# Own tokens' q, g and i as seven block products on two pairs of token blocks, with one written order for five engines

## The chip, the cores and the metric

One Trainium2 chip, one of its cores. The metric is the device time of one launch in microseconds (us); lower is better. TensorE is called PE below, VectorE DVE, ScalarE ACT, GpSimd POOL, and SyncE, whose queue issues most transfers, SP. Matrix work is done in float32 precision by splitting each float32 operand into a high and a low part of a shorter format and adding three products: high times high, high times low, low times high.

## The reference

One layer of a mixed attention and recurrence model on 2048 own tokens and 256 context tokens, width 1024:

```
hx = modulate(rmsnorm(x, g_norm1), mx[0], mx[1])        # (2048, 1024)
hc = modulate(rmsnorm(ctx, g_norm1), mc[0], mc[1])      # (256, 1024)
px = split(hx @ w_in);  pc = split(hc @ w_in)           # w_in: (1024, 3328)
#   columns: q 512, k 128, v 128, hq 512, i 512, ff 512, fb 512, g 512
qx = apply_rope(rmsnorm(heads(px.q), g_q), cos, sin)
kx = apply_rope(rmsnorm(heads(px.k), g_k), cos, sin);  kc = rmsnorm(heads(pc.k), g_k)
att = softmax attention of qx over all keys (context and own)
hg  = bidirectional HGRN2 recurrence of (hq, i, ff, fb), read out with rmsnorm and silu(g)
x = x + mx[2] * (concat(att, hg) @ w_out)
x = x + mx[5] * swiglu(modulate(rmsnorm(x, g_norm2), mx[3], mx[4]), w_gu, w_down)
return rmsnorm(x, g_final)
```

`mx` and `mc` are six vectors each of `silu(c) @ w_mod + b_mod`. The change touches the product with `w_in` and what is done to q and k on the way out of it; the stages behind it stay as they are.

## The kernel before

**Stages.** First comes an opening in which the tokens are loaded, normalised, modulated and transposed into `hT` (features on the partitions, tokens along the row), with high part `hTh` and low part `hTl`. There are five token blocks: block 0 holds the 256 context tokens, blocks 1 to 4 hold 512 own tokens each. Then come the projection steps, one for each group of 256 columns of `w_in`; then attention and recurrence, the output projection, and the feed-forward part (whose first half is already done with seven block products, line 1785).

**A projection step.** `load_raw` (lines 204 to 212) loads 256 columns of all 1024 rows into `ws`. The pool `wst` behind it has one buffer, which the chunks of `w_mod` (`wm`, line 412, 1 MB each) share. `split_w` (lines 214 to 222) makes the high part `wh` on ACT (line 218) and the low part on DVE (line 221) into one of two places that alternate. Then PE runs in one of two forms. `mm_cols` (line 435) holds a 128x128 block of weights and streams tokens: three matmuls of 512 columns for each of the eight row groups (256 columns for the context block). It serves hq and f (the two gate groups ff and fb together). `mm_rows` (lines 438 to 449) holds 128 tokens and streams weights: line 442 sends high and low weights together past `hTh` (512 columns), line 448 the high weights past `hTl` (256 columns). It serves k and v (`kv`), q, g and i. The result is `both` (lines 451 to 454): ACT copies one half out of the accumulator, DVE adds the other.

**Beside the products.** `qk_side` (lines 533 to 605) takes a tile of 128 tokens of q (four heads of one half) or k: it reads the raw product back from DRAM, squares it, sums it (line 553), takes the root on POOL (line 131), multiplies (lines 557 and 558), applies the rotary table (line 567 on DVE four times, line 571 on POOL, line 572), splits high and low (lines 576 and 577), transposes it on PE (line 584) and stores it with two transfers (line 587). `mod_chunk` (lines 409 to 428) makes 256 of the modulation values: a 1 MB load, eight DVE operations `macc` (lines 415 and 417), one matmul, one add, one store. `first_maxima` (lines 607 to 640) finds the first head group's bound for the softmax. A function `pump` moves these along, one step of each at a time, between the product tiles.

**Order.** The opening and block 0 to 4 with kv and hq0 come first. Then the steps are q0, q1, hq1, g0, g1, f0, f1, f2, f3, i0, i1, and in these only PE follows a written order; the others are placed by the scheduler. `first_maxima` runs in i1. Behind i1 the attention stage begins, in which all five engines follow a written order: its first loads are `qa` (line 1144) and `K` (line 1393), its first matmul is `mx` (line 1159).

Of the kernel before, what the change touches and what calls it, by code (L numbers as in the profile page):

```python
# [16 lines left out]
P = 128  # L17
D = 1024
KT = D // P
# [12 lines left out]
NEV = 5  # L32
# [35 lines left out]
def block_kernel(ctx: ExitStack, tc: tile.TileContext, a: dict, out: bass.AP, dbg=None):  # L68
# [24 lines left out]
    s_m0 = dram("s_m0", [4, P])  # L93
    s_att = [dram(f"s_att{j}", [256, T]) for j in range(2)]
# [109 lines left out]
    def load_raw(i, pieces):  # L204

        ws = wst_p.tile([P, KT, 256], F32, tag="wst", name=f"ws{i}")
        o = 0
        for c0, n in pieces:
            nc.sync.dma_start(ws[:, :, o:o + n],
                              a["w_in"][0, :, c0:c0 + n].rearrange("(k p) c -> p k c", p=P))  # L210
            o += n
        return ws

    def split_w(i, ws, wp):

        whl = wp.tile([P, KT, 2, 256], F32R, tag="wh", name=f"wh{i}")
        wh, wl = whl[:, :, 0, :], whl[:, :, 1, :]
        nc.scalar.activation(wh, ws, AF.Copy)
        for q in range(4):
            ks = slice(2 * q, 2 * q + 2)  # L220
            (nc.vector if q % 2 or i > 1 else nc.gpsimd).tensor_tensor(
                wl[:, ks, :], ws[:, ks, :], f32v(wh[:, ks, :]), op=ALU.subtract)
        return wh, wl, whl
# [85 lines left out]
    with proj as st:  # L309
        w_pools = [w_left, w_right]  # L310
        hTp = pool(st, "hT")
        ev = pool(st, "ev", NEV)
        sm = pool(st, "sm", 4)
        sizes = [256, 512, 512, 512, 512]
        hT = [None] * 5
        for b in (4, 3, 1, 2):
            hT[b] = [hTp.tile([P, KT, sizes[b]], F32R, name=f"hT{w}{b}") for w in "hl"]
        ps_mm = pool(st, "ps_mm", 4, PSUM)
        nchunk = [1]
        turned = [None]  # L320

        def load_w(pieces):
# [3 lines left out]
            return split_w(i, load_raw(i, pieces), w_pools[i % 2])  # L326

        first = [early_w]
        with ExitStack() as p1:
            ps_x = pool(p1, "ps_x", 4, PSUM)  # L330
            xh = pool(p1, "xh", 3)
            for gr in list(range(1, NTOK // 256)) + [0]:
                if gr == 0:
                    xp.close()
                    hTc = pool(st, "hTc", side="right")
                    hT[0] = [hTc.tile([P, KT, 256], F32R, name=f"hT{w}0") for w in "hl"]
# [42 lines left out]
                def split_h(kk, hv, eng):  # L379

                    hi = hT[b][0][:, 2 * kk:2 * kk + 2, o:o + 256]
                    hd = nc.scalar.activation(hi, hv, AF.Copy)
                    return hd, eng.tensor_tensor(hT[b][1][:, 2 * kk:2 * kk + 2, o:o + 256], hv, f32v(hi), op=ALU.subtract)
# [14 lines left out]
        ps_t = pool(st, "ps_t", 2, PSUM)  # L398
        ps_q = pool(st, "ps_q", 2, PSUM)
# [3 lines left out]
        gqk = qp.tile([P, 2, 64], F32, name="gqk")  # L403
        nc.sync.dma_start(gqk[:, 0, :], rows_bcast(a["g_q"]))
        nc.sync.dma_start(gqk[:, 1, :], rows_bcast(a["g_k"]))

# [1799 lines left out]
```

## Time and profile before

| what | value |
|---|---|
| median of 3 runs | 3110.42 us (3109.52 to 3111.95) |
| the profiled execution's own time | 3117.9 us |
| its span, first to last instruction | 3116.1 us |
| granted PE clock, mean | 0.996 |
| busy: PE, DVE, ACT, POOL | 99%, 59%, 42%, 51% |
| the 16 DMA engines, mean | 132 GB/s |

PE is busy nearly all the time, so time can be gained by giving it less to do, and is lost wherever something else keeps it waiting. The share of PE at 99% hides that the other engines' load differs from stage to stage. Times in the views are measured from the start of the span. "Idle before" an operation names what ended that idle time.

### The profile page before, as it was taken

The numbers are of one execution on the slowest core, as the hardware profiler recorded it, in microseconds if no ns is written. First come the engines' busy times: TensorE is split into PE (matmuls) and PEld (weight loads), VectorE is DVE, ScalarE is ACT, GpSimd is POOL, SyncE is SP. The second block draws the span as 40 slices with busy tenths as digits, with TensorE's granted clock in tenths as the row PEclk, the third lists the DMA queues.
The fourth block names the chain that finished last, engine by engine and source line by source line (L and its number), as shares of the span: only waits on it lengthen the run. The fifth ranks groups of instructions, "written<-read, shape, count | busy, mean of one in ns | idle before, by whom it ended". The sixth has DMA issues, their size and how long they took to land.

```text
span 3116.1 us, 51235 instructions
## 1 busy us (share of the span) xinstructions
PE 3074.8 (99%) x18844; PEld 2483.8 (80%) x18844; DVE 1845.9 (59%) x3252; ACT 1303.1 (42%) x2656; POOL 1602.7 (51%) x1291
## 2 busy tenths in 40 slices
PE   9999999999999999999999999999999999999999
PEld 7888888886777778777778878788888788888887
DVE  4554655427777787786745574544478743333567
ACT  4422322214545545555553253333345533333454
POOL 3311212106989888898862118676600277776122
PEclk9999999999999999999999999999999999999999
DMA  7544544425111212111124444656596533333765
GB/s 244 159 139 127 155 139 150 141 69 138 42 38 49 67 53 71 39 52 48 42 83 147 129 142 155 213 176 211 171 331 196 182 118 106 102 102 102 254 195 196
DMA packets 372998, 410.77 MB, mean 132 GB/s; under 512 B 34469, under 2 KB 264073, under 8 KB 372234
## 3 DMA queue, kind: packets, MB, share of 16 engines
q1 hardware_dynamic: 369722, 405.06, 41.0%
q8 instruction: 148, 2.42, 0.3%
q10 hardware_dynamic: 3024, 2.43, 0.2%
q14 instruction: 104, 0.85, 0.1%
HBM read 277.54 MB, written 133.97 MB: 132 GB/s over the span
## 4 chain that ended last, share of the span: by engine, by line
PE 70%; DVE 7%; DMA 5%; POOL 3%; issue 2%; ACT 1%; SPq 1%; POOLq 0%; DVEq 0%; ACTq 0%
PE pA L1785 13%; PE av L1215 7%; PE pB L1785 6%; PE y L1355 6%; PE pd0A L2082 4%; PE pd1A L2082 3%; PE s L1190 3%; PE s L1191 3%; PE pC L1785 3%; PE mx L1159 3%; PE i L442 2%; DVE mn L1161 2%; PE pd0B L2082 2%; PE pd1B L2082 2%; PE pa L818 2%
## 5 line engine op out<-in xcount | busy, mean ns | idle before, releaser
L1194 ACT ACTIVATE p<-s 128x512 f32<-128x512 f32 x576 | 338.2, 600 | 372.6 <-PE s L1191 358.1
L1161 DVE TENSOR_REDUCE mn<-mx 128x1 f32<-128x512 f32 x496 | 337.0, 689 | 175.2 <-PE mx L1159 172.3
L1215 PE MATMUL av<-p,VS 128*64 128x256 f32 x2304 | 259.9, 379 | 0.0
L1190 PE MATMUL s<-qa,K 128*128 128x512 f32 x576 | 244.1, 424 | 1.2 <-ACT p L1194 1.0
L1191 PE MATMUL s<-qb,KB 128*128 128x512 f32 x576 | 226.9, 394 | 0.0
L1215 PEld LDWEIGHTS av<-p,VS 128*64 128x64 f32 x2304 | 160.4, 137 | 75.3 <-issue 1.1
L1205 POOL TENSOR_TENSOR ps<-p,p 128x1024 f32<-128x1024 f32 x64 | 153.4, 2396 | 101.8 <-ACT p L1194 101.7
L1159 PE MATMUL mx<-K,qa 128*128 128x512 f32 x496 | 200.1, 404 | 2.4 <-DVE mn L1161 1.2
L435 PE MATMUL f<-hTh,wh 128*128 128x512 f32 (+1 forms) x640 | 188.1, 373 | 0.2 <-ACT ft L475 0.2
L1205 POOL TENSOR_TENSOR ps<-ps,p 128x1024 f32<-128x1024 f32 x64 | 153.1, 2392 | 12.0 <-ACT p L1194 10.6
L2019 DVE TENSOR_TENSOR dl<-dl,x 128x512 fp32r<-128x512 f32 x154 | 113.8, 765 | 66.5 <-ACT x L2012 64.9
L2012 ACT ACTIVATE x<-dl 128x512 fp32r<-128x512 f32 x154 | 95.9, 631 | 95.4 <-DMA dl<-s_hid0S 37.7
L852 POOL TENSOR_TENSOR Q<-Q,T 128x512 f32<-128x512 f32 x96 | 131.3, 1383 | 8.1 <-PE pa L818 7.7
L435 PEld LDWEIGHTS f<-hTh,wh 128*128 128x128 f32 x640 | 116.9, 190 | 20.4 <-ACT ft L475 0.3
L1190 PEld LDWEIGHTS s<-qa,K 128*128 128x128 f32 x576 | 109.0, 189 | 27.0 <-issue 12.3
L2012 ACT ACTIVATE dh<-dl 128x512 fp32r<-128x512 f32 x154 | 88.9, 624 | 98.7 <-PE pd1A L2082 42.2
L2019 DVE TENSOR_TENSOR dl<-dl,dh 128x512 fp32r<-128x512 f32 x154 | 105.5, 697 | 39.9 <-ACT dh L2012 37.7
L1159 PEld LDWEIGHTS mx<-K,qa 128*128 128x128 f32 x496 | 93.6, 189 | 38.0 <-DVE mn L1161 15.3
L131 POOL TENSOR_TENSOR rs_xf<-ms_xf,mhalf 128x1 f32<-128x1 f32 x16 | 9.9, 620 | 221.1 <-DVE ms_xf L129 218.5
L1191 PEld LDWEIGHTS s<-qb,KB 128*128 128x128 f32 x576 | 109.3, 190 | 14.9
L435 PE MATMUL f<-hTl,wh 128*128 128x512 f32 (+1 forms) x320 | 118.7, 371 | 0.0
L131 POOL TENSOR_TENSOR rs_qq<-ms_qq,mhalf 128x4 f32<-128x4 f32 x32 | 34.0, 1061 | 161.0 <-DVE ms_qq L129 160.3
(436 smaller groups left out, 8913.5 us busy)
## 6 DMA issues: line engine op xcount, KB each, us to landing
w<-in_w_gu_dram SPq DMA_DIRECT2D x88, 512.0 KB
wm<-in_w_mod_dram SPq DMA_DIRECT2D x24, 1024.0 KB
dl<-s_wT SPq DMA_DIRECT2D x88, 256.0 KB
dl<-s_wB SPq DMA_DIRECT2D x66, 256.0 KB
wq<-in_w_down_dram SPq DMA_DIRECT2D x44, 256.0 KB
s_wT<-wq SPq DMA_DIRECT2D x44, 256.0 KB
dl<-s_hid1S SPq DMA_DIRECT2D x44, 256.0 KB
dl<-s_hid0S SPq DMA_DIRECT2D x44, 256.0 KB
```

Source lines behind the costliest of these rows:

```text
L435: nc.tensor.matmul(pm[:, :n], w[wi][:, k, c0:c0 + P], hT[b][hi][:, k, :], start=(k == 0 and i == 0), stop=(k == KT - 1 and i == 2))
L1159: nc.tensor.matmul(s, self.qa[:, h * P:(h + 1) * P], K[:, k * 512:(k + 1) * 512], start=True, stop=True)
L1161: nc.vector.tensor_reduce(self.mn[:, h, k:k + 1], s, axis=AX.X, op=ALU.min)
L1190: nc.tensor.matmul(s, KS[self.g][:, ks], self.qa, start=True, stop=False)
L1191: nc.tensor.matmul(s, KB[k // 6][:, k % 6 * P:(k % 6 + 1) * P], self.qb, start=False, stop=True)
L1194: nc.scalar.activation(self.pairs[p][:, o:o + 512], s, AF.Exp, scale=-1.0)
L1205: (nc.gpsimd if SUMS[p] in "PQ" else nc.vector).tensor_tensor(t, a, self.pairs[p], op=ALU.add)
L1215: nc.tensor.matmul(self.av[i * 64:(i + 1) * 64, :256], VS[k // 6][:, k % 6, :], self.pairs[k // 2][:, o:o + 256], start=(k == 0), stop=(k ...
L1355: nc.tensor.matmul(py, m[:, k, :], wo[k][w][hf], start=(k == 0 and i == 0), stop=(k == KT - 1 and i == 2), skip_group_check=True)
L1785: nc.tensor.matmul(acc, w[wi][:, k, :], x[xi][k], start=(start and k == 0 and i == 0), stop=(stop and k == KH - 1 and i == 2), skip_group_ ...
L2019: nc.vector.tensor_tensor(lo, f32v(lo), f32v(hi), op=ALU.subtract)
L2082: nc.tensor.matmul(cur[t], l[:, t * P:(t + 1) * P], r, start=(start and j == 0 and f == 0), stop=(stop and j == NHF - 1 and f == 2), skip_ ...
```

## The change

Own tokens' q, g and i (six groups of 256 columns) are no longer made by `mm_rows` one group at a time. Two groups of 256 columns, the two halves of the 1024 rows and two blocks of 512 tokens form a 2 by 2 by 2 block product, which is done with seven products instead of eight (the scheme that the feed-forward part uses). The weight blocks are A, their sums S1 to S4; the token blocks are B, their sums T1 to T4. Each product has 512 rows of weights, 512 tokens, 256 columns, again in three high and low parts.

- `hT` is now kept as places of half a block (four row groups, 512 tokens, high and low). T1 to T4 take over places of the blocks they are made from, so the raw blocks 1 and 2 are first stored to DRAM (`s_tok`, eight transfers of 1 MB during kv and hq0) and are loaded back when the first pair is done.
- Order of the steps: hq1, f0, f1, f2, then the context's i (two steps of two tiles), then f3, then the first pair (blocks 3 and 4) with q, g, i, then the second (blocks 1 and 2) with q, i, g. Each of these six chunks has seven phases of two slots: 84 slots. A slot is two token tiles of four row groups of three matmuls with 256 columns (line 880).
- From f3 on, PE, DVE, ACT, POOL and SP all follow one written order, built from a table of slots. Weight sums run on POOL (line 838), highs on ACT (line 845), lows on DVE (line 851). Token sums run half on DVE and half on POOL (line 731), with highs on ACT (line 737) and lows on DVE (line 740). They are written for slots -4 to 6 and 38 to 52.
- Results are gathered by an ACT copy (line 967) and DVE adds (line 972). g is finished by Silu on ACT (line 860) and the multiplication by `g_hg` on POOL (line 862). Results are stored from ACT's queue (line 701).
- `g_q`, `g_k` and the constants are multiplied into the rotary table (`gtab`, line 563) once for each tile of 128 tokens, the separate multiplication by `gqk` goes, the four rotary operations on DVE become two (line 580), and the small operation ahead of the root moves to POOL (line 568).
- `first_maxima` runs in the last chunk. The number of evacuation buffers goes from 5 to 4.

Core of the diff:

```diff
-        steps = [None, None,
-                 (jobs_q, 0, ones_of(C_Q)), (jobs_q, 1, ones_of(C_Q + 256)),
-                 (jobs_hq, 1, ones_of(C_HQ + 256)),
-                 (jobs_g, 0, ones_of(C_G)), (jobs_g, 1, ones_of(C_G + 256))]
-        steps += [(jobs_f, h, [(C_FF + h * P, P), (C_FB + h * P, P)]) for h in range(NH)]
-        steps += [(jobs_i, c, ones_of(C_I + c * 256)) for c in range(2)]
+        steps = [(jobs_hq, 1, ones_of(C_HQ + 256))] + [(jobs_f, h, pieces_f(h)) for h in range(NH - 1)]
+        steps += [(context_i, c, ones_of(C_I + c * 256)) for c in range(2)] + [(jobs_f, NH - 1, pieces_f(NH - 1))]
...
+        for i, (f, c, _) in enumerate(steps[:-1]):
+            allowed[0] = 10 + 2 * i
             for n, _ in enumerate(f(c, w)):
...
+                if n == 1:
+                    settle()
                     wn = load_w(steps[i + 1][2])
+                if n >= 1:
+                    pump()
+                    if f is not context_i:
+                        pump()
...
+        chunks = [(pair, ch) for pair, chs in ((1, [chunk_q, chunk_g, chunk_i]), (0, [chunk_q, chunk_i, chunk_g]))
+                  for ch in chs]
+        phases = [("A11", "B11", "A", True, False), ("A12", "B21", "C", True, True), ("S1", "T1", "B", True, False),
+                  ("S2", "T2", "A", False, False), ("S4", "B22", "B", False, True), ("S3", "T3", "A", False, False),
+                  ("A22", "T4", "A", False, True)]
...
+            for t in (2 * u, 2 * u + 1):
+                dst, ts = acc[:, t % 2 * 256:(t % 2 + 1) * 256], slice(t * P, (t + 1) * P)
+                for k in range(H):
+                    for i, (v, f) in enumerate(((vh, 0), (vh, 1), (vl, 0))):
+                        nc.tensor.matmul(dst, v[:, k, ts], w[:, k, f, :],
...
+            summed_at, high_at = (tail_(j - 3), head(j - 2)) if j > 2 else (-4, (-4, 0, 0)[j])
+            if phases[m][0] in SUMS_W:
+                at(summed_at, SUM, weight_sum, c, phases[m][0])
+            at(high_at, HIGH, weight_high, j)
+            at(high_at + 1, LOW, weight_low, j)
...
+        for k in (-4, -4, -3, -3, -2, -2, -1, -1, 0, 1, 2, 3, 4, 5, 6):
+            at(k, TURN, turn)
+        for k, v in ((1, ("B11",)), (3, ("B21",)), (5, ("B12", "T1")), (9, ("B22",))):
+            at(SWITCH + k, LOAD, fetch_tokens, *v)
+        for k in range(10, 25):
+            at(SWITCH + k, TURN, turn)
```

The written order moves instructions at three places that the prediction speaks of.

First, DVE between the context's i and f3. `wh7` and `wh8` are the split weights of two steps that follow each other (`_0` and `_1` are halves), `ws7` and `ws8` the raw ones, `macc16` the modulation chunk that is made from the load `wm16`. Before, at the beginning of f0, where `wh8` serves the next step, f1:

```order
L454 TENSOR_TENSOR ge1_17_4193<-ge1_17_4193,g1_17_4176 128x256
L129 TENSOR_SCALAR ms_qq0_12_4438<-ssq0_12_4436 128x4
L557 TENSOR_TENSOR eq0_12_4416<-eq0_12_4416,rs_qq0_12_4440 128x256
L221 TENSOR_TENSOR wh8_4269<-ws8_4266,wh8_4269 128x2x256 x4
L509 TENSOR_TENSOR ge1_17_4193<-ge1_17_4193,ghg_995 128x256
```

With the change, where `wh7` serves the second step of the context's i and `wh8` serves f3:

```order
L223 TENSOR_TENSOR wh7_1_3416<-ws7_3413,wh7_1_3416 128x2x256 x2
L508 TENSOR_TENSOR macc15_3254<-macc15_3254,pm15_3367 1x256
L375 TENSOR_TENSOR ie0_0_3388<-ie0_0_3388,i0_0_3371 128x256
L375 TENSOR_TENSOR ie0_1_3409<-ie0_1_3409,i0_1_3392 128x256
L495 TENSOR_SCALAR macc16_3467<-wm16_3423,sc_144 128x256
L497 SCALAR_TENSOR_TENSOR macc16_3467<-wm16_3423,sc_144,macc16_3467 128x256 x2
L375 TENSOR_TENSOR ie1_0_3442<-ie1_0_3442,i1_0_3425 128x256
L497 SCALAR_TENSOR_TENSOR macc16_3467<-wm16_3423,sc_144,macc16_3467 128x256 x5
L375 TENSOR_TENSOR ie1_1_3463<-ie1_1_3463,i1_1_3446 128x256
L223 TENSOR_TENSOR wh8_0_3479<-ws8_3476,wh8_0_3479 128x2x256 x2
L223 TENSOR_TENSOR wh8_1_3480<-ws8_3476,wh8_1_3480 128x2x256 x2
```

Between the splits of `wh7` and `wh8` there now stand the four product tiles of the context's i (`ie`) and all of `macc16`; before, a whole step of PE's work stood between two splits, and the chunk was long done.

Second, DVE at the change of pairs. `csq` is a tile's rotary table, `e`, `fx` its values, `sum` the token sum being made, `ws21` a split weight block, `p...` an accumulator. Before, in g0 with q's tiles beside it:

```order
L557 TENSOR_TENSOR eq0_4_3537<-eq0_4_3537,rs_qq0_4_3574 128x256
L417 SCALAR_TENSOR_TENSOR macc14_3484<-wm14_3442,sc_136,macc14_3484 128x256
L454 TENSOR_TENSOR ge0_12_3436<-ge0_12_3436,g0_12_3419 128x256
L558 TENSOR_TENSOR eq0_4_3537<-eq0_4_3537,gqk_997 128x256
L553 TENSOR_REDUCE ssq0_5_3796<-eq0_5_3758 128x4
L567 TENSOR_TENSOR eq0_4_3537<-eq0_4_3537,csq0_4_3539 128x4x16 x2
```

With the change, where the second pair's sums begin:

```order
L731 TENSOR_TENSOR sumh_5442<-vB12h_5235,vB11h_5051 128x1024
L731 TENSOR_TENSOR sumh_5442<-sumh_5442,vB12l_5236 128x1024
L584 TENSOR_TENSOR e1_1027<-e1_1027 128x256
L566 TENSOR_REDUCE ssq1_12_5455<-fx_3954 128x4
L972 TENSOR_TENSOR suml_3846<-pA2_0_4963,suml_3846 128x512
L851 TENSOR_TENSOR ws21_5461<-wr30_5232,ws21_5461 128x4x256
L731 TENSOR_TENSOR sumh_5442<-sumh_5442,vB11l_5052 128x1024
L595 TENSOR_TENSOR sq1_11_5453<-e1_1027,sq1_11_5453 128x256
```

The sums over 1024 elements of a row (`sum`) and the lows of the weights (`ws21`) now stand in one line with the evacuation (`suml` from `pA2`) and the tiles of q.

Third, SP at the end of the stage. `s_q1` are the stores of q's tiles, `K0` the keys that the first matmul of attention reads. Before:

```order
L498 DMA s_i0_66<-ie0_16_6579 128x256
L611 DMA early_6688<-s_k0_74 128x2048
L612 DMA early_6688<-s_k0_74 128x256
L498 DMA s_i0_66<-ie0_17_6600 128x256
L614 DMA early_6688<-s_q0_72 64x512 x2
L1144 DMA qa0_0_7143<-s_q0_72 64x512 x2
L639 DMA s_m0_77<-early_6688 4x128
L1393 DMA K0_7115<-s_k0_74 128x2304
```

With the change:

```order
L658 DMA s_m0_77<-earlyl_6758 4x128
L606 DMA s_q1_73<-sq1_3_7174 64x2x256 x2
L1294 DMA gt04_10612<-s_g0_68 128x4x128
L606 DMA s_q1_73<-sq1_4_7270 64x2x256 x2
L606 DMA s_q1_73<-sq1_5_7326 64x2x256 x2
L1463 DMA qa0_0_7434<-s_q0_72 64x512 x2
L1712 DMA K0_7406<-s_k0_74 128x2304
```

`K0` now stands behind the stores of the last two tiles of q; before, the last stores of q stood some twenty rows ahead of it.

More of the change, by code (lines that the diff above doesn't have):

```diff
@@ new lines, in fetch_tokens, with settle @@
+        def fetch_tokens(n, place=None):
+            V[n] = quarter(place or n, f"v{n}")
+            for w in range(2):
+                nc.sync.dma_start(f32v(V[n][w]), s_tok[n][w])
+        for n, spot in (("B11", (1, 0)), ("B21", (1, 1)), ("B12", (2, 0)), ("B22", (2, 1))):
+            for w_ in range(2):
+                nc.sync.dma_start(s_tok[n][w_], f32v(hT[spot][w_]))
+        def settle():
+            for v in mactive:
+                while not v[1]:
+                    v[1] = next(v[0], 0) == 2
@@ L707, in block_kernel @@
+        for k in range(END, END + 4):
+            run(k, 99)
+        while side or active:
+            pump()
         order.close()
```

630 lines of the change are left out of this document (420 added, 210 removed).

## The prediction

> **What bounds the kernel now.** I read the page first, then stretches of the projection stage by time, then PE's timeline, then the groups of instructions by shape.
>
> ```profile
> PE 3074.8 (99%) x18844; PEld 2483.8 (80%) x18844; DVE 1845.9 (59%) x3252; ACT 1303.1 (42%) x2656; POOL 1602.7 (51%) x1291
> ```
>
> ```profile
> core 0: us, PE busy (x) PEld busy (x) DVE busy (x) ACT busy (x) POOL busy (x), PEclk, DMA share, GB/s
> ...
> 41.00:152.00 111.00, 109.30 (x607) 93.23 (x608) 61.74 (x129) 60.64 (x123) 48.37 (x45) 1.00 0.50 158
> 152.00:245.50 93.50, 93.50 (x536) 79.94 (x536) 51.55 (x183) 24.01 (x65) 15.66 (x22) 1.00 0.46 141
> ...
> 386.00:603.00 217.00, 214.50 (x1074) 176.01 (x1073) 119.15 (x353) 59.96 (x116) 47.62 (x47) 0.99 0.49 148
> 603.00:709.50 106.50, 106.50 (x610) 92.48 (x609) 29.66 (x63) 18.42 (x43) 6.19 (x14) 1.00 0.30 97
> ```
>
> The rows are kv and hq0, then q, f and i. PE is busy through all of them and nothing else is near its limit: DVE 51.6 of 93.5 us in q, POOL 15.7. So PE's work is the bound here, and a step that fills DVE and POOL starts with room.
>
> **The products.** PE's timeline in q (one row of 128 tokens against 256 columns: a pair of lines 442 and 448), and in f on the context block, where each matmul of 256 columns has its own weights as the new products do:
>
> ```profile
> 159.69 0.40 PE L442 MATMUL q<-wh,hTh 128*128 128x512 f32 x1
> 159.93 0.28 PE L448 MATMUL q<-wh,hTl 128*128 128x256 f32 x1
> 160.04 0.40 PE L442 MATMUL q<-wh,hTh 128*128 128x512 f32 x1
> 160.28 0.28 PE L448 MATMUL q<-wh,hTl 128*128 128x256 f32 x1
> 160.39 0.40 PE L442 MATMUL q<-wh,hTh 128*128 128x512 f32 x1
> ```
>
> ```profile
> 386.77 0.28 PE L435 MATMUL f<-hTl,wh 128*128 128x256 f32 x1
> 386.89 0.40 PE L435 MATMUL f<-hTh,wh 128*128 128x256 f32 x2
> 387.13 0.28 PE L435 MATMUL f<-hTl,wh 128*128 128x256 f32 x1
> ```
>
> Starts, not durations, give the cost, since matmuls overlap. A pair takes 160.39 - 160.04 = 0.35 us; a matmul of 256 columns takes (387.13 - 386.77) / 3 = 0.12 us. Before, six groups of 16 tiles and 8 row groups are 768 pairs: 768 x 0.353 = 271.1 us. After, 84 slots of 24 matmuls are 2016 x 0.120 = 241.9 us. **Saving 29.2 us**, a little under the eighth that seven products for eight would give (33.9), because 0.12 x 3 is more than 0.353. The context's i, the transposes of q's tiles, hq and f cost PE what they did.
>
> **The way into f3.** In the old order a modulation load between two weight loads had a whole step to hide in. Now `ws7` (second context step), `wm16` and `ws8` (f3) go through the one buffer of `wst` while PE has only the context's i.
>
> ```profile
> 159.99 0.60 SPq L412 DMA_DIRECT2D wm<-in_w_mod_dram  x1
> ```
>
> ```profile
> 166.59 0.35 DVE L415 TENSOR_SCALAR macc<-wm,sc 128x256 f32<-128x256 f32 x1 [4.79 <-DMA wm<-in_w_mod_dram]
> ```
>
> ```profile
> 439.12 1.02 SPq L209 DMA_DIRECT2D ws<-in_w_in_dram  x2
> ```
>
> ```profile
> L218 ACT ACTIVATE wh<-ws 128x2048 fp32r<-128x2048 f32 x13 | 24.8, 1910 | 4.8 <-DMA ws<-in_w_in_dram 4.8
> ...
> L475 ACT ACTIVATE ft<-f 128x512 f32<-128x512 f32 x32 | 20.1, 627 | 48.6 <-DMA s_f<-ft 48.6
> L585 ACT ACTIVATE sq<-pq 128x512 fp32r<-128x512 f32 x32 | 18.8, 589 | 0.0
> ```
>
> `wh7` goes to the place that f2 reads, so its split starts when f2 ends. From there: split 3.0 us (1.91 and the last lows), `wm16` 166.59 - 159.99 = 6.6, the eight `macc` 0.35 + 7 x 0.48 = 3.7, `ws8` another 6.6, its first half split 1.6: 21.5 us. PE has four context tiles of 8 pairs, 32 x 0.353 = 11.3 us. It waits 10.2, and the clock's ramp after it adds about one: **+11**. Bounds: transfers of 4.5 us on emptier queues give 7, one like the issue at 439.12, whose split begins at 447.3, gives 13.
>
> **DVE and POOL beside the products.** The costs by shape:
>
> ```profile
> L417 DVE SCALAR_TENSOR_TENSOR macc<-wm,sc,macc 128x256 f32<-128x256 f32 x112 | 53.9, 481 | 1.5
> ...
> L572 DVE TENSOR_TENSOR eq<-eq 128x256 f32<-128x256 f32 x32 | 13.5, 422 | 13.8 <-POOL eq L571 13.8
> ...
> L594 DVE TENSOR_TENSOR skNone<-ekNone,skNone 128x128 fp32r<-128x128 f32 x18 | 5.2, 288 | 9.0 <-ACT skNone L593 8.9
> ...
> L1205 DVE TENSOR_TENSOR ps<-ps,p 128x1024 f32<-128x1024 f32 x1 | 1.2, 1224 | 0.1
> ```
>
> ```profile
> L383 POOL TENSOR_TENSOR hTl<-h,hTh 128x512 fp32r<-128x512 f32 x25 | 33.2, 1345 | 33.1 <-ACT hTh L382 33.1
> L571 POOL TENSOR_TENSOR eq<-eq,csq 128x256 f32<-128x256 f32 x32 | 30.7, 960 | 70.4 <-DVE eq L567 58.7 <-ACT eq L551 4.3 <-DVE ms_qq L129 3.2
> ...
> L1205 POOL TENSOR_TENSOR ps<-p,p 128x1024 f32<-128x1024 f32 x2 | 4.8, 2407 | 21.5 <-ACT p L1194 21.5
> ```
>
> Neighbours on DVE start closer than their durations:
>
> ```profile
> 160.54 0.41 DVE L454 TENSOR_TENSOR qe<-qe,q 128x256 f32<-128x256 f32 x1
> 160.87 0.28 DVE L572 TENSOR_TENSOR ekNone<-ekNone 128x128 f32<-128x128 f32 x1
> ```
>
> 0.33 us from one to the next for a duration of 0.41, so 0.08 comes off each. From the first token sum on, DVE has 36 sums and lows of T and 42 lows of weights of 1024 elements, 78 x 1.14 = 89 us; for 32 tiles of q three operations of 256 (0.34) and three of 128 (0.21), 53; 49 `macc`, 20: 162 us, all with both inputs in SBUF. POOL has 44 of 1024 (2.4 us) = 105, 32 of 256 (about 0.75, between the 0.46 of 128 elements below and the mean of 0.96) = 24, 15 of 512 (1.3) = 20: 149. PE has there 242, four transposes of at most 0.12 for each of the 32 tiles, under 15, half of f3 (217 / 8) 27 at most and the first maxima 18 x 0.3 = 5: about 285. Alone, each fits. Together they do not seem free of each other:
>
> ```profile
> 156.68 2.49 DVE L221 TENSOR_TENSOR wh<-ws,wh 128x512 fp32r<-128x512 f32 x4
> ```
>
> ```profile
> 156.78 2.74 POOL L571 TENSOR_TENSOR ekNone<-ekNone,cskNone 128x128 f32<-128x128 f32 x1 [0.95 <-ACT qe L453]
> 160.01 0.46 POOL L571 TENSOR_TENSOR ekNone<-ekNone,cskNone 128x128 f32<-128x128 f32 x1 [0.49 <-DVE ekNone L567]
> ```
>
> ```profile
> L1755 DVE TENSOR_TENSOR A11l<-w,A11h x44: 679/1358/1784, 1819.0 to 2836.8; 128x512 fp32r<-128x512 f32 x44
> ...
> L1755 DVE TENSOR_TENSOR S1l<-S,S1h x2: 681/687/693, 1831.0 to 1856.9; 128x512 fp32r<-128x512 f32 x2
> ```
>
> The same POOL operation takes 0.46 us alone and 2.74 us when DVE's four lows run from 156.68 to 159.17: it ends 0.35 us after they do. In the feed-forward part one low on DVE takes 0.68 at best, 1.36 in the middle, 1.78 at most. So they exclude each other, and the demand is 162 + 149 = 311 us, 26 over PE's 285. It is uneven: most in g (tiles of q and `macc` beside POOL's g) and in the change of pairs, where ten sums of 1.1 and 2.25 us meet loads that land a slot late; least in i. Some POOL work meets DVE's operations on PSUM, so I take **+20**, bounds 0 (all of it overlaps) and 26. The rest is hidden: the multiplication by `gqk` that goes (32 x 0.42 on DVE), one more table load on ACT, longer rotary tables.
>
> The Trainium skill, "SBUF — State Buffer", section "SBUF: two separate sides", says that the pair of ports that DVE and GpSimd share is an exclusive lock held for the whole instruction, and that a DVE operation with two SBUF inputs takes it against a GpSimd operation that reads SBUF. The rows agree (0.46 against 2.74 us). By that rule the term is its upper bound or more; the forecast would be 6 us later or worse.
>
> **The last tiles of q.** They now end the stage, behind g on ACT, and `K` waits on SP behind their stores.
>
> ```profile
> L1393 SPq DMA_DIRECT2D K<-s_k x1: 332/332/332, 700.1 to 700.1; - x1
> ```
>
> ```profile
> L1144 SPq DMA_DIRECT2D qa<-s_q x2: 451/520/588, 700.5 to 701.0; - x2
> ```
>
> ```profile
> L587 SPq DMA_DIRECT2D s_q<-sq x8: 574/580/600, 600.3 to 620.7; - x8
> ```
>
> ```profile
> 709.34 0.28 PE L448 MATMUL i<-wh,hTl 128*128 128x256 f32 x1
> 709.45 0.64 PE L1159 MATMUL mx<-K,qa 128*128 128x512 f32 x2
> 711.15 1.10 PE L1159 MATMUL mx<-K,qa 128*128 128x512 f32 x2 [1.05 <-DVE mn L1161]
> ```
>
> Before, `K` was issued at 700.1 and `mx` followed i without a gap. After, from the end of the last product: Silu 0.63, POOL's multiplication 1.3, for which ACT's queue waits (its store) with the last tile behind it; high and low 0.84, transposes 0.38, copy 0.59, two stores 1.16, two `qa` 1.04, `K` issued 0.33 and landed about 6 later (1152 KB; the rows allow up to 709.45 - 700.15 = 9.3): **+12**, bounds 8 and 15.
>
> **Eight stores of 1 MB** in kv and hq0 stand ahead of x loads on SP. Between 41 and 152 us the DMA share is 0.50 and PE waits 1.7 us: **+2**, bounds 0 and 10.
>
> **Sum.** -29.2 + 11 + 20 + 12 + 2 = +15.8 us on the profiled execution's 3117.9 us (span 3116.1). That execution lies 7.5 us over the median; the terms are differences, so I set them on the median: 3110.4 + 15.8 = 3126.
>
> **Rivals.** (A) *Covered.* DVE and POOL overlap enough, or POOL's operations mostly meet DVE's reads of PSUM, so the products run at PE's pace. It decides where the demand that really excludes stays under 285 us, that is if 26 of the 149 us of POOL meet no two-input operation. The last g is then not late on POOL and the tail falls to 8: -29.2 + 11 + 0 + 8 + 2 = -8, 3102. For it: POOL's 15.7 and DVE's 51.6 us of 93.5 in q leave gaps, and the feed-forward part, with the same sums, keeps PE at 99%. Against: that demand. (B) *Locked throughout.* DVE's queue is in order, so evacuations from PSUM stand behind a blocked operation, and the products wait for their accumulators. DVE's 162, the 36 adds from PSUM and 18 reductions (some 0.7 each, 38) and POOL's 149 in one line would be 349, 64 over; between 26 and 64 I take 45: -29.2 + 11 + 45 + 12 + 2 = +41, 3151. For it: the middle value of 1.36 for a low of 0.68. Against: PE's 99% there. This is the outcome that the section of the Trainium skill's page "SBUF — State Buffer" cited above would lead one to expect. (C) *No saving*: a matmul of 256 columns with weights changed every time runs at 0.134 us, which is where 2016 of them take the old 271: -29.2 + 29 and the other terms, 3155. f's rows at 0.12 speak against it.
>
> **Chances.** Forecast 0.50, A 0.33, B 0.15, C 0.02. Range: 3097 leaves out A's lower third (0.1), 3152 about half of B and all of C (0.1). Within 0.2% (6.2 us, about what a measurement of this kernel can tell from no change) lie a third of A (0.11) and 0.06 of the forecast, another 0.02 of which is faster: same 0.17; faster 0.22 + 0.02 = 0.24; slower 0.59.
>
> **What would show it.** In the profile after: 2016 matmuls of line 880 starting 0.12 us apart within a slot; PE idle about 10 us just ahead of f3, released by the lows of `wh8`, with `wm16` landing between; PE waits of some 20 us in all within the 84 slots, mostly on DVE's lows or adds, thickest in the g chunk and at slots 38 to 54, with DVE's 1024-element operations well over 1.2 us; `K` issued after the last product and `mx` some 12 us behind it. A PE that runs on through the 84 slots makes it A; waits of over 35 us there make it B; a gap ahead of f3 or `mx` of under 4 us, or over 20, breaks that term.

## The result, and the profile after

The changed kernel takes 3205.18 us (median of 4 runs, 3202.74 to 3206.66) against 3110.2 us before: a ratio of 1.0304, with an interval of 1.0286 to 1.0322. The direction was forecast. The time was not: it lies 79 us above the 3126 of the forecast and 53 above the end of the range.

The profiled execution spans 3203.7 us against 3116.1. The page's line of busy times, after:

```profile
PE 3076.6 (96%) x19324; PEld 2517.4 (79%) x19324; DVE 1970.8 (62%) x3081; ACT 1339.4 (42%) x2652; POOL 1747.0 (55%) x1401
```

There are 480 matmuls more (2016 for 1536), so the products are there. The account in two numbers: PE idle was 3116.1 - 3074.8 = 41.3 us and is 3203.7 - 3076.6 = 127.1, **85.8 more**. PE busy should have fallen by the 29.2 us of the forecast and rose by 1.8, so **31.0 us** have to be explained there as well. The two spans differ by 87.6 us and the medians by 95, because the profiled execution of the kernel before lies 7.5 us over its median; this account is one of the spans.

The stage by stretches of time, after. The last two columns are the share of the DMA engines and GB/s; the one ahead of them is the granted clock:

```profile
core 0: us, PE busy (x) PEld busy (x) DVE busy (x) ACT busy (x) POOL busy (x), PEclk, DMA share, GB/s
...
41.00:152.00 111.00, 109.78 (x610) 93.94 (x611) 64.19 (x131) 60.23 (x124) 45.74 (x47) 1.00 0.66 233
...
300.00:350.00 50.00, 50.00 (x247) 41.52 (x246) 16.31 (x38) 10.11 (x22) 1.35 (x3) 1.00 0.37 127
...
550.00:600.00 50.00, 32.55 (x236) 31.39 (x236) 34.77 (x55) 10.88 (x21) 22.49 (x18) 0.83 0.79 270
600.00:650.00 50.00, 40.74 (x294) 39.45 (x295) 44.44 (x39) 19.30 (x28) 34.19 (x16) 0.86 0.35 110
```

Up to f2 (300 to 350) PE is full at full clock, and the eight stores of 1 MB between 41 and 152 cost nothing. In the 84 slots (425 to 782) PE is idle for 5 to 17 us out of 50, the granted clock is 0.83 to 0.93, and DVE is busy for up to 44 of 50, where the q stage before had it at 51.6 of 93.5. Who PE waited for between f3 and the first `mx` (us in all, times, longest):

```profile
PE pq L602 <- DVE sq L595: 24.3, 7, 12.0
PE pA L880 <- DVE suml L972: 13.9, 5, 4.8
PE pq L602 <- DVE small L634: 10.6, 4, 6.5
PE mx L1478 <- DMA qa<-s_q: 10.6, 1, 10.6
PE f L356 <- ACT wh L220: 8.4, 1, 8.4
PE pA L880 <- DVE ws L851: 6.7, 2, 4.0
PE pq L602 <- ACT sq L593: 5.7, 2, 5.2
PE pC L880 <- ACT ws L845: 5.2, 1, 5.2
```

The waits ahead of f3 (8.4) and of `mx` (10.6, and 5.2 for the last tile of q) add up to about what was forecast for the two (11 with the clock, and 12). The rest, some 66 us, is waiting inside the 84 slots, 57 of it put down to DVE: to the lows of q's tiles (24.3), which PE must transpose in its written order, to adds that free an accumulator (13.9), to the reductions of the first maxima (10.6) and to lows of weights. The DVE groups between 380 and 800 us (mean ns of one behind the busy time):

```profile
L497 DVE SCALAR_TENSOR_TENSOR macc<-wm,sc,macc 128x256 f32<-128x256 f32 x49 | 39.4, 805 | 1.1
L851 DVE TENSOR_TENSOR ws<-wsum,ws 128x1024 fp32r<-128x1024 f32 x24 | 35.4, 1477 | 15.2 <-ACT ws L845 15.2
L584 DVE TENSOR_TENSOR fx<-fx 128x256 f32<-128x256 f32 x16 | 24.2, 1510 | 3.7 <-POOL fx L582 3.0
...
L584 DVE TENSOR_TENSOR e<-e 128x256 f32<-128x256 f32 x16 | 19.5, 1218 | 3.3 <-POOL e L582 3.1
```

Line 584 adds 256 elements, which took 422 ns before; now 1510 and 1218. One of them, on DVE and on POOL:

```profile
567.03 2.62 DVE L584 TENSOR_TENSOR fx<-fx 128x256 f32<-128x256 f32 x1 [0.71 <-POOL fx L582]
```

```profile
566.27 0.73 POOL L582 TENSOR_TENSOR fx<-fx,csq 128x256 f32<-128x256 f32 x1 [2.35 <-DVE fx L580]
566.96 2.41 POOL L838 TENSOR_TENSOR wsum<-wr,wr 128x1024 f32<-128x1024 f32 x1
```

It waits for POOL's rotary multiplication, which ends at 567.0. POOL's next operation, a sum of weights, starts in the same instant and runs to 569.4; DVE's addition, 0.42 us of work before, ends at 569.65. The Trainium skill, "SBUF — State Buffer", section "SBUF: two separate sides", calls this a lock held for the whole instruction, with the loser fully blocked, and the rows agree (2.62 us against 0.42).

The half clock, in f3's first matmuls behind its wait (three matmuls of 256 columns from 373.50 to 374.14, 0.64 us; before, 0.36):

```profile
372.18 0.58 PE L356 MATMUL f<-hTch,wh 128*128 128x256 f32 x1 [8.37 <-ACT wh L220]
...
373.50 0.42 PE L356 MATMUL f<-hTcl,wh 128*128 128x256 f32 x1
...
374.14 0.41 PE L356 MATMUL f<-hTcl,wh 128*128 128x256 f32 x1
```

The trace records when the clock was halved. Over the whole execution PE is busy for some 74 us at half clock, against 20 before. If half of such time is lost, that is 37 against 10, and the 27 between them are most of the 31.0 us.

### The profile page after: what moved, and what is told of

Its sections match the earlier page's. It is cut to its first block, busy times and chain, and to the rows that moved or that the text cites. A ratio compares the mean times of both kernels' runs of the same rounds, so it can differ in the third digit from the quotient of the medians.

```text
span 3203.7 us, 51844 instructions
## 1 busy us (share of the span) xinstructions
PE 3076.6 (96%) x19324; PEld 2517.4 (79%) x19324; DVE 1970.8 (62%) x3081; ACT 1339.4 (42%) x2652; POOL 1747.0 (55%) x1401
## 4 chain that ended last, share of the span: by engine, by line
PE 64%; DVE 6%; DMA 3%; POOL 2%; issue 2%; ACT 1%; SPq 0%; POOLq 0%; ACTq 0%; DVEq 0%
PE pA L2104 12%; PE av L1534 7%; PE pB L2104 6%; PE y L1674 5%; PE pd0A L2401 4%; PE s L1509 3%; PE pd1A L2401 3%; PE s L1510 3%; PE pC L2104 3%; PE mx L1478 3%; DVE mn L1480 2%; PE pd0B L2401 2%; PE pd1B L2401 2%; PE pa L1137 2%; PE av L1542 2%
## 5 line engine op out<-in xcount | busy, mean ns | idle before, releaser
L1478 PE MATMUL mx<-K,qa 128*128 128x512 f32 x496 | 200.5, 406 | 12.3 <-DMA qa<-s_q 10.6
L2368 POOL TENSOR_TENSOR y<-y,yg 128x512 f32<-128x512 f32 x24 | 40.6, 1707 | 144.8 <-DVE yg L2367 94.5
L2104 PE MATMUL pB<-x,S1h 128*128 128x512 f32 x352 | 110.3, 395 | 3.2 <-ACT S1h L2073 3.2
L2074 DVE TENSOR_TENSOR A11l<-w,A11h 128x512 fp32r<-128x512 f32 x44 | 60.7, 1379 | 83.6 <-ACT A11h L2073 83.6
L2104 PE MATMUL pA<-x,S3h 128*128 128x512 f32 x352 | 109.6, 392 | 1.9 <-DVE x L1984 1.3
```

Source lines behind the costliest of these rows:

```text
L1478: nc.tensor.matmul(s, self.qa[:, h * P:(h + 1) * P], K[:, k * 512:(k + 1) * 512], start=True, stop=True)
L2104: nc.tensor.matmul(acc, w[wi][:, k, :], x[xi][k], start=(start and k == 0 and i == 0), stop=(stop and k == KH - 1 and i == 2), skip_group_ ...
```

## The experiments

Theory L, formed from these rows: DVE and POOL exclude each other on operations with both inputs in SBUF; POOL's sums stretch DVE's queue; PE waits on it in its written order, and runs at half clock behind each longer wait. The rivals: DVE is late because of transfers that it waits for, or simply because it has too much to do. Each ratio is to the kernel before on the same chip; where nothing else is said, an interval is about 0.003 to each side.

**POOL's sums left out.**

```diff
-            for ks, eng in halves:
+            for ks, eng in halves[:1]:
...
-            return wsum[:, SUMS_W[name][2]] if name in SUMS_W else raw(c, name[1:])
+            return raw(c, "22") if name in SUMS_W else raw(c, name[1:])
...
-            nc.gpsimd.tensor_tensor(source(c, name), part(x), part(y), op=op)
+            return
...
-                    nc.gpsimd.tensor_tensor(r4, r4, ghg[:, None, :].to_broadcast([P, 4, P]), op=ALU.mult)
```

> Changed kernel, but in the 84 slots POOL's sums of weights, POOL's half of the token sums and POOL's multiplication of g by g_hg are left out (the highs and lows read a raw weight block and the other half of the sum in their place; the result is not the layer's). DVE, ACT, PE and all transfers keep their work; POOL keeps the rotary multiplication and the root. Theory L (DVE is late because POOL and DVE exclude each other on operations with two SBUF inputs): DVE's mean for the lows of 1024 elements falls to 1.22 us and for line 584 to 0.42, PE's waits in the slots fall from 73 us to under 30, time near 3130. Rival M (DVE is late because its queue stands behind the small transfers of the modulation chunks): the 12 us wait at 585 and most others stay, time above 3180.

Ratio 1.0073 (1.0047 to 1.0100): 2.3%, some 72 us, of the 3.0% are gone. DVE's groups in this run:

```profile
L851 DVE TENSOR_TENSOR ws<-wr,ws 128x1024 fp32r<-128x1024 f32 x42 | 51.2, 1221 | 24.1 <-ACT ws L845 24.0
L497 DVE SCALAR_TENSOR_TENSOR macc<-wm,sc,macc 128x256 f32<-128x256 f32 x49 | 26.9, 548 | 1.1
L584 DVE TENSOR_TENSOR fx<-fx 128x256 f32<-128x256 f32 x16 | 6.7, 422 | 2.8 <-POOL fx L582 2.4
```

The lows of weights and line 584 are back at the duration of an undisturbed operation (1.22 and 0.42 us); `macc`, at 548 ns, is nearly so (481 before). With the same 3081 operations DVE is busy for 80 us less (1891.0 for 1970.8). Of the waits that stay in the slots, one of 14.4 us for a tile of q belongs to the first rival: DVE itself stands 12.0 us for a small transfer (`s_mod`) just ahead of it.

**The same POOL work, for nobody.** The run above also takes away that others wait for POOL's results. So POOL does as many operations of the same size into a scratch place:

```diff
-            for ks, eng in halves:
-                eng.tensor_tensor(x[:, ks], y[:, ks], z[:, ks], op=op)
+            nc.vector.tensor_tensor(x[:, :2], y[:, :2], z[:, :2], op=op)
+            spare_pool(8)
...
+        def spare_pool(n):
+            g = ghg[:, None, :].to_broadcast([P, n, P])
+            nc.gpsimd.tensor_tensor(wsum[:, 0].rearrange("p k c -> p (k c)")[:, :n * P].rearrange("p (h v) -> p h v", v=P), g, g, op=ALU.mult)
...
-            nc.gpsimd.tensor_tensor(source(c, name), part(x), part(y), op=op)
+            nc.gpsimd.tensor_tensor(wsum[:, o], part(x), part(y), op=op)
...
-                    nc.gpsimd.tensor_tensor(r4, r4, ghg[:, None, :].to_broadcast([P, 4, P]), op=ALU.mult)
+                    spare_pool(4)
```

> As the run that leaves POOL's sums out, but POOL does as many operations of the same size again (44 of 1024 elements, 16 of 512, both inputs in SBUF) into a scratch place that nobody reads; nobody waits for them. The result is not the layer's. It tells whether POOL's sums cost time because others wait for their results (then near the run without them, ratio to before 1.01 or less) or because DVE is blocked while they run (theory L: ratio 1.02 or more, DVE's operations stretched as in the changed kernel).

Ratio 1.0291. Nobody reads these sums, and the time is back. DVE is busy for 1972.5 us, as in the changed kernel (1970.8), and line 584 is stretched again:

```profile
L584 DVE TENSOR_TENSOR fx<-fx 128x256 f32<-128x256 f32 x16 | 26.6, 1665 | 4.3 <-POOL fx L582 3.4
L584 DVE TENSOR_TENSOR e<-e 128x256 f32<-128x256 f32 x16 | 24.2, 1515 | 3.0 <-POOL e L582 2.9
```

So POOL's results coming late are not needed for the loss; that POOL is in an operation is enough. One dependence stays in this run: the loads of the next weight blocks wait until POOL has read the last ones (SP stands 19.1 us for it here, 29.4 in the changed kernel, 0 in the run without sums). What that costs was not separated.

**All sums on DVE.**

```diff
-halves = [(slice(0, 2), nc.vector), (slice(2, 4), nc.gpsimd)]
+halves = [(slice(0, 2), nc.vector), (slice(2, 4), nc.vector)]
...
-            nc.gpsimd.tensor_tensor(source(c, name), part(x), part(y), op=op)
+            nc.vector.tensor_tensor(source(c, name), part(x), part(y), op=op)
...
-                    nc.gpsimd.tensor_tensor(r4, r4, ghg[:, None, :].to_broadcast([P, 4, P]), op=ALU.mult)
+                    nc.vector.tensor_tensor(r4, r4, ghg[:, None, :].to_broadcast([P, 4, P]), op=ALU.mult)
```

> Changed kernel with POOL's 44 sums of 1024 elements and 16 multiplications of 512 done on DVE. DVE gets 44 x 1.14 + 16 x 0.6 = 60 us more of its own work. Theory L: POOL's 125 us of blocking go, and DVE's stretch of some 78 us with them, so DVE's queue is shorter than before by about 20 us: faster than the changed kernel by 15 to 40 us, 3165 to 3190 against its 3205. Rival (DVE is the engine that is too full, whatever POOL does): slower than the changed kernel by 40 us or more.

Ratio 1.0261, span 3191.1: 13 us faster (the two intervals just touch), though DVE has 60 us more of its own work. From the first product to the last, after and in this run:

```profile
425.00:790.00 365.00, 292.22 (x2183) 282.14 (x2181) 285.67 (x399) 126.16 (x214) 199.81 (x163) 0.89 0.47 147
```

```profile
425.00:776.00 351.00, 289.17 (x2182) 279.64 (x2180) 262.51 (x457) 128.38 (x215) 84.13 (x109) 0.90 0.49 154
```

58 operations more, and DVE is busy for 23 us less. The rival "too full, whatever POOL does" asked for 40 us more, and falls in that form. But PE still waits nearly as long, so the lock is not all: with this much in DVE's order, PE waits for it either way.

**The rotary multiplication on DVE**, for q.

```diff
-                nc.gpsimd.tensor_tensor(x, x, cs[:, 0, None, :].to_broadcast([P, nh, 64]), op=ALU.mult)
+                (nc.vector if isq else nc.gpsimd).tensor_tensor(x, x, cs[:, 0, None, :].to_broadcast([P, nh, 64]), op=ALU.mult)
```

> Changed kernel with the rotary multiplication of q's tiles (line 582, 256 elements) on DVE instead of POOL. DVE gets 32 more operations of 0.34 us, 11 us in all; POOL loses 32. Theory L: line 584 no longer comes right behind a POOL operation whose successor starts at once and blocks it, so its mean falls from 1.36 to about 0.6 us (30 us off DVE's queue), time lower by 10 to 30. Rival (DVE is simply too full): time higher by 5 to 15.

Ratio 1.0302, no change, where 10 to 30 us less were expected, though line 584 is freed:

```profile
L595 DVE TENSOR_TENSOR sq<-e,sq 128x256 fp32r<-128x256 f32 x16 | 26.7, 1667 | 0.0
...
L584 DVE TENSOR_TENSOR e<-e 128x256 f32<-128x256 f32 x16 | 7.5, 467 | 0.0
```

The block went to operations that come later while POOL is in a sum, above all the lows of q's tiles (566 ns in the changed kernel, 1667 here). DVE's busy time did not fall (1986.5 for 1970.8, of which some 11 are the added work).

**Which sums.** Weight sums alone left out, and POOL's half of the token sums alone.

```diff
-            return wsum[:, SUMS_W[name][2]] if name in SUMS_W else raw(c, name[1:])
+            return raw(c, "22") if name in SUMS_W else raw(c, name[1:])
...
-            nc.gpsimd.tensor_tensor(source(c, name), part(x), part(y), op=op)
+            return
```

> Changed kernel with only POOL's 24 sums of weight blocks left out (highs and lows read a raw block in their place; the result is not the layer's). Theory L, by POOL's time: 24 of 44 sums and 16 multiplications, 58 of 125 us, so about half of the 71 us that all of them cost: 30 to 40 us less, ratio 1.019.

```diff
-            for ks, eng in halves:
+            for ks, eng in halves[:1]:
...
-                nc.scalar.activation(v[0][:, ks], x[:, ks], AF.Copy)
+                nc.scalar.activation(v[0][:, ks], x[:, :2], AF.Copy)
...
-                nc.vector.tensor_tensor(v[1][:, ks], x[:, ks], f32v(v[0][:, ks]), op=MINUS)
+                nc.vector.tensor_tensor(v[1][:, ks], x[:, :2], f32v(v[0][:, ks]), op=MINUS)
```

> Changed kernel with only POOL's half of the token sums left out (20 operations; ACT and DVE read the other half in its place; the result is not the layer's). Theory L by POOL's time: 48 of 125 us, 25 to 30 us less, ratio 1.021, all of it at the start and at the change of pairs. The two runs and the 16 multiplications should come to about 71.

Ratios 1.0206 and 1.0209, 0.98% and 0.95%: about 30 us each. Together that is 60 of 72; the rest, for the 16 multiplications by `g_hg` and what the parts do to each other, was not measured alone.

**The modulation chunks.** In the changed kernel DVE waits 10 us at 583 for one of their small transfers, and PE 12 us for DVE:

```profile
582.75 0.35 DVE L495 TENSOR_SCALAR macc<-wm,sc 128x256 f32<-128x256 f32 x1 [10.06 <-DMA s_mod<-macc]
```

```profile
585.15 0.50 PE L602 MATMUL pq<-identr,sq 128*128 128x128 f32 x2 [11.98 <-DVE sq L595]
```

First all chunks ahead of the 84 slots:

```diff
-            allowed[0] = 10 + 2 * i
+            allowed[0] = min(12 + 4 * i, 24)
...
+                        for _ in range(3):
+                            mod_pump()
```

> Changed kernel with the modulation chunks 8 to 23 all done in hq1 and f0 to f2, none beside the context's i and none in the 84 slots. The work is the same. Theory L: DVE loses 36 us of macc (16 of them spent blocked) and 21 us of waiting for small transfers in the slots, but the operations of q's tiles stay stretched: the gap ahead of f3 goes (8), the slots' waits fall from 73 to about 50, time 3205 - 8 - 23 - about 10 of clock = 3165. Rival M: the slots' waits fall below 30, time near 3130.

Ratio 1.0297, no change. The wait ahead of f3 and the one at 585 are gone and the slots' waits fell to 54 us, about as L expected (50), but the gain was given back, nearly all of it in the steps where the chunks now stand. Two of eight such waits, which make 29 us in all:

```profile
204.17 1.01 PE L503 MATMUL pm<-macc,ones 128*1 128x256 f32 x2 [6.03 <-DVE macc L497]
...
225.15 1.01 PE L503 MATMUL pm<-macc,ones 128*1 128x256 f32 x2 [6.35 <-DVE macc L497]
```

Each chunk ends in a matmul in PE's written order, and that matmul now comes before DVE has made `macc`. Then only the small transfers moved to ACT's queue:

```diff
-            nc.sync.dma_start(row, a["b_mod"][:, j * 256:(j + 1) * 256])
+            (nc.scalar if j > 17 else nc.sync).dma_start(row, a["b_mod"][:, j * 256:(j + 1) * 256])
...
-            nc.sync.dma_start(modrow[:1, j * 256:(j + 1) * 256], row)
+            (nc.scalar if j > 17 else nc.sync).dma_start(modrow[:1, j * 256:(j + 1) * 256], row)
```

> Changed kernel with the two small transfers of modulation chunks 18 to 23 (a row of b_mod in, the finished row out) on ACT's queue instead of SP's, where one of them stands behind four token blocks of 1 MB and DVE waits 10 us for it (PE 12 us at 585). If that wait is a loss of its own, 12 to 18 us less with the half clock behind it: 3187 to 3193, ratio 1.025. If DVE's backlog from POOL's blocking takes its place, within 5 us of the changed kernel.

Ratio 1.0265, span 3197.8: 6 us by the spans, 12 by the ratio, whose intervals touch. PE's wait there fell from 12.0 to 7.0 us. What keeps the 7.0 was not tested; the expectation named DVE's backlog.

**The way into f3.** Chunks 8 to 17 done ahead of the context's i.

```diff
-            allowed[0] = 10 + 2 * i
+            allowed[0] = min(11 + 4 * i, 18)
...
+                        for _ in range(2):
+                            mod_pump()
```

> Changed kernel with modulation chunks 8 to 17 done before the context's i and none beside it, so that ws8 follows ws7 through the one buffer. Chunks 18 to 23 stay where they were. The gap of 8.4 us ahead of f3 goes; with the half clock behind it 10 to 14 us less, 3191 to 3195. If the gap were given back in the slots, time would stay within 4 us of 3205.

Ratio 1.0272 (1.0231 to 1.0313), span 3193.9. The gap is gone. The ratio is 10 us lower, but the intervals overlap and the two executions lie 10 us apart, so a gain is not shown. Six waits ahead of the chunks' matmuls in the earlier steps, 12 us in all, stand against it (five for `macc`, 6.5; one put down to ACT, 5.4).

**The end.** One more step of q's tiles in every second slot of the chunk ahead of the last.

```diff
+            if n % 2 and FINAL - 14 <= n < FINAL:
+                at(n, SIDE, pump)
```

> Changed kernel with one more step of q's tiles in every second slot of the chunk ahead of the last, so that the last tiles of q are stored before the last product ends and the load of K stands behind nothing. The waits of 5.2 and 10.6 us at the end shrink to about 6 in all, 8 to 12 us less, if DVE has room for the tiles in that chunk; if it is as full there as elsewhere, the waits come up there and the time stays within 4 us of 3205.

Ratio 1.0303. The waits ahead of `mx` fall from 15.8 to 6.6 us, those for DVE and ACT in the chunk where the tiles now run (640 to 735) grow from 10.6 to 17.3, and PE's idle time as a whole stays (126.4 for 127.1). DVE has no room for them there either.

**The rotary table alone**: the kernel before, with g_q and g_k in the table, the rotation as in the changed kernel, and four evacuation buffers.

```diff
-        gqk = qp.tile([P, 2, 64], F32, name="gqk")
+        gtab = qp.tile([P, 2, 2, 64], F32, name="gtab")
...
+                nc.vector.tensor_tensor(cs, cs, gtab[:, 0 if isq else 1], op=ALU.mult)
...
-            nc.vector.tensor_tensor(x, x, gqk[:, 0 if isq else 1, None, :].to_broadcast([P, nh, 64]),
-                                    op=ALU.mult)
```

> The kernel before with one part of the change alone: g_q and g_k folded into the rotary table, two rotary operations on DVE instead of four, the small operation ahead of the root on POOL, four evacuation buffers. The products stay as they were. By the prediction's sum this part is hidden: ratio 0.998 to 1.002.

Ratio 1.0011 (1.0000 to 1.0023): hidden, as the prediction said. By the interval at most 7 of the 95 us can be its, as far as the order before tells.

**Four edits together**: all sums on DVE, the small transfers on ACT's queue, the way into f3, the end. The core of each, from the diffs above:

```diff
+            (nc.scalar if j > 17 else nc.sync).dma_start(row, a["b_mod"][:, j * 256:(j + 1) * 256])
...
+        halves = [(slice(0, 2), nc.vector), (slice(2, 4), nc.vector)]
...
+            allowed[0] = min(11 + 4 * i, 18)
...
+            if n % 2 and FINAL - 14 <= n < FINAL:
```

> Changed kernel with four edits together: all sums and the multiplication by g_hg on DVE, chunks 8 to 17 ahead of the context's i, the small transfers of the others on ACT's queue, one more step of q's tiles in every second slot of the chunk ahead of the last. If the losses add up (10 for the way into f3, 13 for DVE, some 12 for the small transfers, some 5 at the end) 40 us below the changed kernel: 3165, ratio 1.0175. If the same time is counted twice, 3180.

Ratio 1.0232 (1.0182 to 1.0282), 0.7% below the changed kernel where the four alone add up to 1.15% (0.43, 0.39, 0.32 and 0.01): so the gains do not add up, though the interval leaves room for it. PE still waits for DVE's adds (8.6 us at 488, 9.5 at 598).

**The account.** No sums on POOL, and the other three losses mended:

```diff
+            (nc.scalar if j > 17 else nc.sync).dma_start(row, a["b_mod"][:, j * 256:(j + 1) * 256])
...
+            for ks, eng in halves[:1]:
...
+            allowed[0] = min(11 + 4 * i, 18)
...
+            if n % 2 and FINAL - 14 <= n < FINAL:
```

> Changed kernel without POOL's sums and its multiplication by g_hg (as in the first of these runs; the result is not the layer's) and with the three other losses mended: chunks 8 to 17 ahead of the context's i, the small transfers of the others on ACT's queue, one more step of q's tiles in every second slot ahead of the last chunk. If the account is complete (POOL's blocking 71, way into f3 10, small transfers some 14, end some 6), the saving on PE shows: the run without POOL's sums had a ratio of 1.0073, so 23 us, less 30: ratio 0.996 to 1.000. If something else is still missing, above 1.004.

Ratio 1.0060 (1.0037 to 1.0083), and not under 1. Without the three mends it was 1.0073, so they gave nothing that can be told from the spread. The page's line of this run, span 3129.0:

```profile
PE 3055.6 (98%) x19324; PEld 2496.7 (80%) x19324; DVE 1889.5 (60%) x3081; ACT 1339.9 (43%) x2652; POOL 1607.3 (51%) x1341
```

PE is busy for 19.2 us less than before. It is busy at half clock for 29 us against 20, which takes back 4.4 of the saving, so PE's work fell by some 24 us here; the same estimate gives 25 for the changed kernel and 28 for the run without POOL's sums, against the 29.2 of the forecast. PE is idle for 73.4 us, 32 more than before. Of that, 13 us are waits ahead of the chunks' matmuls in the early steps, 7 ahead of `mx`, 4.2 for an add at the change of pairs, and the rest small ones. By its own sign (above 1.004) the expectation failed: the mended waits came up again in other places, and the account is not closed. Even without POOL's sums the written order spends the saving.

**PE kept busy through its two longest waits.**

```diff
+        for _ in range(64):
+            nc.tensor.matmul(pf[:, :256], hT[0][0][:, 0, :P], hT[0][0][:, 0, :], start=True, stop=True)
...
+        for _ in range(140):
+            nc.tensor.matmul(pf[:, :P], identr, identr, start=True, stop=True)
```

> Changed kernel with PE given matmuls that nobody reads where it waits longest: 64 of 256 columns ahead of f3 and 140 of 128 columns ahead of the first mx. They fit into the two waits (8.4 and 10.6 us), so that PE does nothing later for them. If the half clock behind a wait is the wait's doing, f3 and mx start at full clock: 3 us less at f3 and 4 to 8 at mx, ratio 1.027 to 1.028. If the clock stays low there all the same, 1.030 or more.

Ratio 1.0366, slower, because the 140 small matmuls took 0.215 us each and ran some 19 us past the wait that they were to fill. What was asked shows ahead of f3:

```profile
362.64 7.83 PE L937 MATMUL fill<-hTch 128*128 128x256 f32 x64
371.16 0.39 PE L356 MATMUL f<-hTch,wh 128*128 128x256 f32 x1 [0.69 <-ACT wh L220]
...
372.93 0.28 PE L356 MATMUL f<-hTcl,wh 128*128 128x256 f32 x1
373.05 0.40 PE L356 MATMUL f<-hTch,wh 128*128 128x256 f32 x2
373.29 0.28 PE L356 MATMUL f<-hTcl,wh 128*128 128x256 f32 x1
```

From 372.2 on three take 0.36 us, where the changed kernel needed 0.64 until 378, and the granted clock is 1.00 from 363 to 431. So the half clock is the wait's doing; it cost f3 about 2.9 us by the rows (half of the 5.8 from 372.2), and from the last matmul of i to the first product the run is 2.3 us shorter.

## Why the prediction was wrong

The steps in their order. **The products**: right in the main; within a slot they start 0.12 us apart, and with the half clock taken off PE's work fell by 24 to 28 us of the 29.2. What the others are stays open. **The way into f3**: right, 8.4 us of wait and 2.9 of half clock for the forecast 11, with `wm16` between the two loads. (The wait ended with a high on ACT, not with the lows of `wh8` as was said.) **The last tiles of q**: the place was right, `K` issued at 792.3 and the first `mx` at 799.4; the waits, 5.2 and 10.6, make 15.8 for 12 forecast, just over the bound of 15, and the trace puts the end of the longer one down to `qa`, issued just ahead of `K`. **The eight stores**: nothing for 2. **The rotary table**: hidden, right.

**"DVE and POOL beside the products", +20**, is the step that failed. Its mechanism was right and was shown: the two engines exclude each other, and with POOL's long operations gone 72 us go. Its size was read off wrongly. The text added up what excludes (162 + 149 = 311 us), compared it with PE's 285 and took the surplus of 26 as an upper bound. That would hold if the work could be spread freely over the section. It can't: each engine follows its written order, each operation has its slot, PE's transposes and accumulators depend on DVE's results a slot or two later, and a wait is not made up in a slot with room. What counts is the 80 us by which DVE's own operations are stretched, and where. Some 66 us of PE's waits came of this and of the transfers below, far over the 35 that the prediction gave as the sign of rival B. Rival B was the nearest: it named the waits for accumulators behind a blocked operation (13.9 us), but not the larger ones for the tiles of q (24.3), and took 45 for the term. The rule from the Trainium skill, "SBUF — State Buffer", section "SBUF: two separate sides", which the prediction cited as making it "6 us later or worse", deserved the weight of the forecast.

**A term was missing**: the half clock. The forecast put "about one" behind the gap ahead of f3, where 2.9 came, and nothing behind any other wait. With two dozen waits in 365 us PE was granted 0.89 of its clock there, and the recorded half clock explains 27 of the 31.0 us that the account lacked. Only for f3's wait was it shown by an experiment that the wait is the cause.

**A wait was missing**: DVE behind the small transfers of the modulation chunks, while four token blocks of 1 MB were on SP's queue. The prediction spoke of the loads landing late, not of the short row behind them; 12 us of PE at 585, of which 5 could be had back.

## What to carry to other kernels

Moving work from TensorE to VectorE and GpSimd is not free because both have idle time: operations of the two with both inputs in SBUF run one after the other, so a POOL operation of 2.4 us can put up to 2.4 us on any such DVE operation that meets it, however short (2.62 us for 0.42 here). Where every engine follows a written order and the consumer is a slot away, price this as the stretch of each DVE operation at its place, not as the surplus of a sum over the section, and give each wait of PE its half clock as well. An eighth off a stage that is 9% of the kernel promised 29 us; measured against that, the waits and the half clock that came with it cost some 117 (85.8 and 31.0).

## What the runs showed of the hardware

Behind the wait of 8.4 us PE ran at half clock for 5.8 us. In the record the clock falls 4 us into that wait, at 368.0, and returns at 378.2. Ahead of `mx` it falls at 787.8 and returns at 808.3, 9 us after the first `mx`. But that is hardly the wait's doing: the kernel before had no such wait there, and still ran at half clock for 6.8 us behind its first `mx`, where short waits for DVE lie between the matmuls:

```profile
713.00:719.00 6.00, 5.78 (x11) 3.39 (x12) 4.80 (x7) 0.60 (x1) 0.00 (x0) 0.50 1.10 265
```

How long the half clock lasts depends on what PE does then. In the run with the fillers, 140 matmuls of 128 columns (the identity by itself, with a weight load for each), one behind the other for 30 us, left the granted clock where it was:

```profile
790.00:800.00 10.00, 10.00 (x49) 10.00 (x49) 0.00 (x0) 0.00 (x0) 0.00 (x0) 0.50 0.94 256
800.00:810.00 10.00, 10.00 (x49) 10.00 (x49) 0.00 (x0) 0.00 (x0) 0.00 (x0) 0.50 0.81 204
```

PE counts as busy all the time and gets 0.50. Full clock came only 12 us after larger matmuls followed, of which the first 7 had short waits between them (6.08 us busy of 7) and the last 4.8 had none. The Trainium skill, "TensorE: Matmul & The Clock Gate", section "Part 1: The HAM clock gate (the "warmup" mystery)", puts the return at about 3.4 us of sustained activity, counted in a free-running window. The 10.2 us around f3's wait, from 368.0 to 378.2, fit three such windows, the last of them filled by f3's matmuls. The other stretches of half clock in the changed kernel fit as well: but for the one at its very end they are one to six times 3.4 us long. The 30 us with these small matmuls don't, and there the measurement decides.
